# Turning the rows of a second FFN's Strassen groups back in single pieces, and reordering its last weight splits and output groups

## The chip, the cores and the metric

The kernel runs on one core of one Trainium2 chip. The metric is the device time of one execution in microseconds. The work is spread over TensorE (PE; its weight loads are shown apart as PEld), VectorE (DVE), ScalarE (ACT), GpSimd (POOL) and SyncE (SP), which issues most of the DMAs. Each engine runs its own instructions strictly in the order in which the program wrote them, and waits on semaphores for the others.

## The reference, cut to what matters

One decoder layer over 512 tokens of width 1024: a gated FFN, a mixer of attention branches, a second gated FFN, a norm. All in float32. The change is in the second FFN (`norm_ffn2`, `ffn2_gate`, `ffn2_up`, `ffn2_down`, width 2816) and the final norm.

```python
def _rmsnorm(x, g):
    xf = x.astype(jnp.float32)
    y = xf * lax.rsqrt(jnp.mean(xf * xf, axis=-1, keepdims=True) + RMS_EPS)
    return (y * g.astype(jnp.float32)).astype(x.dtype)

def _swiglu(x, w_gate, w_up, w_down):
    return (jax.nn.silu(x @ w_gate) * (x @ w_up)) @ w_down
...
        h = h + FFN_HALF * _swiglu(_rmsnorm(h, norm_ffn2[i]), ffn2_gate[i], ffn2_up[i], ffn2_down[i])
    return _rmsnorm(h, norm_final)
```

## The kernel before

**Products.** A float32 product is three matmuls on rounded (`fp32r`) halves: each operand is split into a high part, a cast on ACT, and a low part, the operand minus the high part, on DVE. The three matmuls are high x high, high x low, low x high.

**Weights.** `Weights` streams all weights in blocks of 128 x 1024. `load` (L143, SP's queue) brings a block into one of four `raw` buffers, free once the block four before it is split. `high` (L151, ACT) and `low` (L155, DVE) split it into one of four slots of `whi` and `wlo`, free once the matmuls of the block four before it are done. `next` hands out block i and, ahead of its matmuls, issues the split of block i + 2; `prep(n)` issues all splits up to block n.

**The second FFN** (L1755 on) has 22 tiles of 128 hidden columns in three parts: tiles 0 to 7, 8 to 16, 17 to 21. Most tiles compute gate and up with 24 matmuls each (`mm3`), then `gated` (Silu(gate) x up). Tiles 8 to 11, 12 to 15 and 17 to 20 are done four at a time by `four`: a Strassen scheme of seven products in the order `FOUR_ORDER` = 1, 5, 6, 3, 7, 2, 4, each of two weight blocks, 12 matmuls a block, with sums of earlier products added as each ends. After the first and second part, `down` multiplies by the down weights, again by Strassen, in 14 steps of one weight block; its left operands are seven matrices a pair of tiles, four of them sums, stored split in `G` (high) and `left` (low). The last part's down product is `finish`: four row tiles of two output groups (three for the last), each a sum of six products with the last six weight blocks, called 0 to 5 here, in the order 0, 1, 4, 5, 2, 3; then the final norm and the output.

**Turning back.** `four` leaves its result with tokens on the partitions, in tiles `s` (list `u`, first token half) and `t` (list `w`, second half); the down product needs hidden columns there. So PE transposes them into PSUM banks `tp` (`turned`) and ACT copies them out. A group hands what is left of this to the list `turns`, and `turn_back` issues one entry at chosen places in what follows. For a group whose result goes to `down`: `pair_rows(u)` is issued at the group's end, and three entries remain: `pair_rows(w)`, then `operands_of(0)` and `operands_of(1)`, each of which forms four sums in the tile `g` (L1918 to L1921) and splits them and one more matrix (L1922 to L1925). For the last group, four entries `whole(n)` each turn and split one tile. `later` holds gating operations (L1850) that are issued after the next `W.next()`.

**Three places** are named in what follows. *Seam 1*: from the end of the group of tiles 8 to 11 through the first products of the group of tiles 12 to 15. *Seam 2*: from the end of that group through tile 16 into `down`. *Tail*: the end of the group of tiles 17 to 20, tile 21, and `finish`. PSUM has two banks each of `acc`, `o`, `s` and `tp`. Blocks 0 and 1 of the last six have storage of their own (`apart`); blocks 2 to 5 take the ring's slots.

In the main loop (L2055 on), a plain tile 21 ran `next(last)` (one step of `finish`) ahead of its gate product and again after its up product:

```python
                if third == 2:
                    settle(later)
                    next(last)
                pg = acc(False)
                ...
                mm3(pu, W.next(), u_in, KD, rows if f == 0 else (lambda: back(third)) if third else None)
```

Of the kernel before, what the change touches and what calls it, by code (L numbers as in the profile page):

```python
# [195 lines left out]
def flat(t):  # L196
    return t.rearrange("p a b -> p (a b)")
# [165 lines left out]
def layer(ctx, tc, a, out):  # L363
# [335 lines left out]
    def mm3(ps, w, x, n, amid=None):  # L699
        (wh, wl), (xh, xl) = w, x  # L700
        for k in range(n):
            if amid is not None and k == n * 3 // 4:
                amid()
            mm(ps, wh[:, k], xh(k), k == 0, False)
            mm(ps, wh[:, k], xl(k), False, False)
            mm(ps, wl[:, k], xh(k), False, k == n - 1)
# [1045 lines left out]
    with pool("temp3", 2) as temp, pool("end") as end:  # L1752
# [24 lines left out]
        def gated(pg, pu, j, pairs):  # L1777
            z = temp.tile([128, S], F32, name="z")
            vector.tensor_tensor(z, pg, r_b, op=OP.mult)
            s = temp.tile([128, S], F32, name="s")  # L1780
            scalar.activation(s, z, AF.Silu)
            t = temp.tile([128, S], F32, name="t")
            vector.tensor_tensor(t, pu, r_b, op=OP.mult)
            if not pairs:
                g = temp.tile([128, 8, 256], F32, name="g", bufs=1).rearrange("p m c -> p (m c)")[:, :S]
                vector.tensor_tensor(g, s, t, op=OP.mult)
                split(*rows_of(j), g)
                return
            if j % 2 == 0:
                left["g"] = temp.tile([128, 8, 256], F32, name="g", bufs=1)  # L1790
            g, p = left["g"], j // 2
            o = g[:, 1:3] if j % 2 else g[:, 0:8:7]
            vector.tensor_tensor(o, *(x.rearrange("p (i c) -> p i c", i=2) for x in (s, t)), op=OP.mult)
            if j % 2 == 0:
                return
            if j == 7:
                W.prep(W.pos + 3)
            operands(g, p)
# [34 lines left out]
        def four(j, pairs):  # L1833
# [1 line left out]

            home = {1: "acc", 2: "acc", 5: "s", 3: "s", 6: "o", 7: "o", 4: "o"}
            slot = {5: 0, 7: 1, 6: 2, 3: 3}
            p, u, w, z = [], [], [], []
            made = {1: (p, "z"), 5: (w, "t"), 6: (u, "s"), 2: (z, "y")}
            col, minus = norm["col"], norm["minus"]  # L1840
            banks = {}
# [10 lines left out]
            for m in FOUR_ORDER:  # L1852
# [3 lines left out]
                for kk in range(2):  # L1856
                    wh, wl = (x.rearrange("p (a b) c -> p a (b c)", a=2) for x in W.next())
                    settle(later)
                    for t in range(2):
                        c, ps = slice(t * 128, t * 128 + 128), banks[home[m]][t]  # L1860
                        for k in range(2):
                            ah, al = (x[:, c] for x in operand(m, 2 * kk + k))
                            for step, (x, y) in enumerate(((ah, wh), (al, wh), (ah, wl))):
                                tensor.matmul(ps, x, y[:, k], start=new and kk == k == step == 0,  # L1864
                                              stop=kk == k == 1 and step == 2, skip_group_check=True)
                    if m == 1 and kk == 1 or m == 5:
                        turn_back()
                if m == 3:
                    next(steps, None)
                if m == 3 and not pairs:  # L1870
# [27 lines left out]
                    tensor.transpose(ps[:, i], x[:, n * 128:n * 128 + 128], ident)  # L1898
                return ps

            def pair_rows(x, first):

                banks = [turned([(x[t], 2 * q + n) for n in range(2) for t in range(2)]) for q in range(2)]
                for q, ps in enumerate(banks):
                    scalar.copy(x[q], flat(ps))
                if first:
                    for q, ps in enumerate(banks):
                        hi, lo = (y[:, j // 2 + q, 0:2] for y in (left_hi, left["lo"]))
                        scalar.copy(flat(hi), x[q])
                        vector.tensor_tensor(flat(lo), x[q], f32(flat(hi)), op=OP.subtract)  # L1910

            def operands_of(q):

                hi, lo = left_hi[:, j // 2 + q], left["lo"][:, j // 2 + q]
                a11, a12 = u[q][:, :256], u[q][:, 256:]
                a21, a22 = w[q][:, :256], w[q][:, 256:]
                g = temp.tile([128, 8, 256], F32, name="g", bufs=1)
                vector.tensor_tensor(g[:, 3], a21, a22, op=OP.subtract)  # L1918
                vector.tensor_tensor(g[:, 5], a11, a21, op=OP.subtract)
                vector.tensor_tensor(g[:, 4], g[:, 3], a11, op=OP.subtract)  # L1920
                vector.scalar_tensor_tensor(g[:, 6], a12, -1.0, g[:, 4], op0=OP.mult, op1=OP.subtract)  # L1921
                scalar.copy(hi[:, 2], a22)  # L1922
                scalar.copy(hi[:, 3:7], g[:, 3:7])
                vector.tensor_tensor(lo[:, 2], a22, f32(hi[:, 2]), op=OP.subtract)
                vector.tensor_tensor(lo[:, 3:7], g[:, 3:7], f32(hi[:, 3:7]), op=OP.subtract)  # L1925

            def whole(n):
                ps = turned([(x, n) for x in (*u, *w)])
                split(*rows_of(j + n), flat(ps))

            if pairs:
                pair_rows(u, True)
                turns.append(lambda: pair_rows(w, False))
                for q in range(2):
                    turns.append(lambda q=q: operands_of(q))
            else:
                for n in range(4):
                    turns.append(lambda n=n: whole(n))
# [45 lines left out]
        def residual(d):  # L1984
# [3 lines left out]
                tensor.transpose(ps[:, t], h[:, d, t * 128:(t + 1) * 128], ident)  # L1988
            scalar.copy(o_t[:, :, d * 128:(d + 1) * 128], ps)

        def finish():


            W.prep(base + 1)
            W.load(base + 5)
            yield
            for j in (4, 5, 2):
                W.split(base + j, 0, 8)
            yield
# [1 line left out]
            for t in range(4):  # L2001
# [3 lines left out]
                last = len(groups) - 2  # L2005
                for half, (c0, c1) in enumerate(zip(groups, groups[1:])):
                    cs = slice(c0, c1)
                    ps = acc(False)[:, :c1 - c0]
                    for n, b in enumerate(LAST_ORDER):
                        j = LAST_ROWS[b]  # L2010
                        wh, wl = (w.rearrange("p k c -> p (k c)")[:, cs] for w in W.place(base + b))
                        gh, gl = (x[:, ts] for x in rows_of(j))
                        mm(ps, gh, wh, n == 0, False)
                        mm(ps, gl, wh, False, False)
                        mm(ps, gh, wl, False, n == 5)
                    y = o_t[:, t, cs]
                    vector.scalar_tensor_tensor(y, ps, 0.5, y, op0=OP.mult, op1=OP.add)
                    sq = temp.tile([128, 512], F32, name="z")
# [41 lines left out]
        for third, (f0, f1) in enumerate(TILES):  # L2060
            if third == 2:
                make_room_again()
            for f in range(f0, f1):
                if any(x <= f < x + 4 for x in FOURS):
# [2 lines left out]
                        next(steps, None)  # L2067
                        turn[0] = 2
                    continue
                if third == 2:  # L2070
                    settle(later)
                    next(last)
                pg = acc(False)
                wp = W.next()
                settle(later)
                mm3(pg, wp, u_in, KD, col if f == 0 else None)
                back(third)
                pu = acc(False)
                mm3(pu, W.next(), u_in, KD, rows if f == 0 else (lambda: back(third)) if third else None)
                if f < 2:  # L2080
                    for d in range(4 * f, 4 * f + 4):
                        residual(d)
                if f == 1:
                    make_room()
                if third == 2:
                    next(last)
                if third < 2 and f + 1 == f1:
                    W.prep(W.pos + 2)
                if third:
# [35 lines left out]
```

## Time and profile before

| | us |
|---|---|
| median of 3 runs | 1125.27 (1123.21 to 1126.33) |
| the profiled execution's own time | 1124.9 |
| its span | 1123.2 |
| mean granted TensorE clock | 0.993 |
| chain that ended last, PE's share | 89% |

The span runs from the first to the last instruction that the profiler saw; the execution's time is 1.7 us longer. In the table of stretches the granted clock is a share of full speed. In a timeline, a matmul's length is modelled and overlaps the next one; the step from start to start (0.227 to 0.233 us for 512 columns at full clock) is its cost. A bracket `[1.90 <-ACT whi L151]` says that the engine was idle for 1.90 us before the row and that ACT's instruction of line 151 on `whi` ended it.

### The profile page before, as it was taken

The page shows a single profiled execution, that of the slowest core. Times are in us where ns is not written, and L with a number is a line of the kernel's source. Part 1 is how long each engine was busy: PE and PEld are TensorE (multiplying, and loading weights), DVE is VectorE, ACT ScalarE, POOL GpSimd, SP SyncE. Part 2 cuts the span into 40 slices and gives each one's busy share as a digit, 9 for nine tenths or more (in the row PEclk, how much of TensorE's full clock was granted, in tenths as well). Part 3 has the DMA queues.
Part 4 walks back from the last instruction along what each step waited for, and adds up shares of the span by engine and source line. Part 5 has one row for each costly group of instructions (what it writes and reads, how often), then busy time and mean ns, then how long its engine had stood idle before and what let it go on. Part 6 is the DMA issues. An engine that isn't in the chain of part 4 may idle for free.

```text
span 1123.2 us, 15782 instructions
## 1 busy us (share of the span) xinstructions
PE 1097.0 (98%) x5835; PEld 935.7 (83%) x5835; DVE 753.5 (67%) x1360; ACT 527.1 (47%) x966; POOL 213.3 (19%) x245
## 2 busy tenths in 40 slices
PE   9999999999999999999999999999999998999987
PEld 7888899988888998898888888888887786777866
DVE  5656777854656588977777466555778767587653
ACT  5433344542434457667667543434345445444432
POOL 0211110000002136645434432131100000000002
PEclk9999999999999999999999999999999999999999
DMA  7988979798656464459979756439998655445612
GB/s 213 258 207 229 237 173 267 227 315 263 210 193 188 104 188 125 139 151 242 320 164 332 173 165 207 123 97 249 266 253 259 203 172 152 148 150 190 204 38 76
DMA packets 203205, 220.90 MB, mean 197 GB/s; under 512 B 7700, under 2 KB 160088, under 8 KB 202840
## 3 DMA queue, kind: packets, MB, share of 16 engines
q1 hardware_dynamic: 177208, 156.84, 45.4%
q0 software_dynamic: 23456, 58.72, 22.7%
q10 hardware_dynamic: 2464, 4.33, 1.0%
q8 instruction: 46, 0.75, 0.3%
q14 instruction: 31, 0.25, 0.1%
HBM read 199.94 MB, written 78.64 MB: 248 GB/s over the span
## 4 chain that ended last, share of the span: by engine, by line
PE 89%; DVE 5%; ACT 3%; issue 2%; DMA 0%; POOLq 0%; DVEq 0%; ACTq 0%; SPq 0%
PE acc L387 30%; PE o L387 20%; PE s L387 20%; PE o L1864 3%; PE o L783 3%; PE s L1864 2%; PE acc L1864 2%; PE tp L1640 2%; PE s L783 2%; PE acc L783 2%; DVE wlo L155 1%; ACT whi L151 1%; PE tp L387 1%; DVE turn_a L1338 0%; DMA raw<-in_cmp_k_w_dram 0%
## 5 line engine op out<-in xcount | busy, mean ns | idle before, releaser
L155 DVE TENSOR_TENSOR wlo<-raw,whi 128x1024 fp32r<-128x1024 f32 (+2 forms) x219 | 252.0, 1173 | 61.3 <-ACT whi L151 61.0
L151 ACT CAST whi<-raw 128x1024 fp32r<-128x1024 f32 (+2 forms) x244 | 222.1, 937 | 102.2 <-PE acc L387 17.4
L387 PE MATMUL acc<-uh,whi 128*128 128x512 f32 x240 | 96.0, 400 | 0.0
L387 PE MATMUL acc<-uh,wlo 128*128 128x512 f32 x240 | 93.9, 391 | 0.0
L387 PE MATMUL acc<-ul,whi 128*128 128x512 f32 x240 | 93.7, 391 | 0.0
L387 PE MATMUL acc<-whi,uh 128*128 128x256 f32 x224 | 65.8, 294 | 1.2 <-ACT whi L151 1.2
L387 PE MATMUL acc<-wlo,uh 128*128 128x256 f32 x224 | 63.6, 284 | 0.1
L387 PE MATMUL acc<-whi,ul 128*128 128x256 f32 x224 | 63.6, 284 | 0.0
L387 PE MATMUL o<-uh,whi 128*128 128x512 f32 x144 | 57.4, 399 | 0.6 <-ACT whi L927 0.6
L1655 DVE TENSOR_TENSOR pts<-tp,pts 128x512 fp32r<-128x512 f32 (+1 forms) x62 | 41.9, 687 | 21.6 <-ACT pts L1652 21.0
L387 PE MATMUL o<-ul,whi 128*128 128x512 f32 x144 | 56.2, 390 | 0.0
L387 PE MATMUL o<-uh,wlo 128*128 128x512 f32 x144 | 56.1, 390 | 0.0
L387 PEld LDWEIGHTS acc<-uh,wlo 128*128 128x128 f32 x240 | 45.0, 188 | 10.2 <-DVE wlo L155 0.4
L2025 POOL TENSOR_TENSOR o_t<-o_t,g_b 128x512 f32<-128x512 f32 (+1 forms) x5 | 5.9, 1179 | 243.6 <-ACT z L2019 243.6
L387 PEld LDWEIGHTS acc<-ul,whi 128*128 128x128 f32 x240 | 45.2, 188 | 8.2
L387 PEld LDWEIGHTS acc<-uh,whi 128*128 128x128 f32 x240 | 45.1, 188 | 8.1
L1554 ACT ACTIVATE pbuf<-s,m 128x256 f32<-128x256 f32 (+3 forms) x96 | 47.6, 503 | 7.6 <-DVE c L1564 3.7
L387 PE MATMUL acc<-G,whi 128*128 128x512 f32 x164 | 50.5, 389 | 0.0
L387 PE MATMUL s<-uh,whi 128*128 128x512 f32 x128 | 49.9, 390 | 0.0
L387 PE MATMUL s<-ul,whi 128*128 128x512 f32 x128 | 49.8, 389 | 0.0
L387 PE MATMUL s<-uh,wlo 128*128 128x512 f32 x128 | 49.8, 389 | 0.0
L387 PE MATMUL s<-G,whi 128*128 128x512 f32 x160 | 49.4, 390 | 0.0
(468 smaller groups left out, 2936.2 us busy)
## 6 DMA issues: line engine op xcount, KB each, us to landing
raw<-in_ffn_gate_dram SPq DMA_DIRECT2D x42, 512.0 KB, 5.0
raw<-in_ffn_down_dram SPq DMA_DIRECT2D x34, 512.0 KB, 5.4
raw<-in_ffn_up_dram SPq DMA_DIRECT2D x32, 512.0 KB, 7.6
t<-in_ffn_down_dram POOLq DMA_DIRECT2D x12, 1024.0 KB, 10.0
w<-in_ffn_up_dram POOLq DMA_DIRECT2D x12, 1024.0 KB, 11.3
raw<-w SPq DMA_DIRECT2D x24, 512.0 KB, 4.0
raw<-in_w_in_dram SPq DMA_DIRECT2D x20, 512.0 KB, 5.1
raw<-s SPq DMA_DIRECT2D x16, 512.0 KB, 5.7
```

The source lines that it names most:

```text
L151: self.nc.scalar.copy(self.place(i)[0][:, k0:k1], self.raw[i][:, k0:k1])
L155: engine.tensor_tensor(lo, self.raw[i][:, k0:k1], f32(hi), op=OP.subtract)
L387: tensor.matmul(out, lhsT, rhs, start=start, stop=stop)
L783: tensor.matmul(o, a_[:, n], x(k), start=new and n == step == 0, stop=n == 7 and step == 2, skip_group_check=True)
L1554: scalar.activation(u.p[:, hd], b.view[:, j], AF.Exp, bias=u.m[:, hd:hd + 1], scale=-1.0, accum_out=u.sum[:, hd:hd + 1])
L1640: tensor.transpose(ps[:w, hd], u.p[:, hd, kb * w:kb * w + w], ident)
L1655: vector.tensor_tensor(p.lo, flat(b.ps)[:w], f32(p.hi), op=OP.subtract)
L1864: tensor.matmul(ps, x, y[:, k], start=new and kk == k == step == 0, stop=kk == k == 1 and step == 2, skip_group_check=True)
L2025: gpsimd.tensor_tensor(y, y, left["g_b"][:, cs], op=OP.mult)
```

## The change

It does seven things, all in the second FFN. (1) Nothing is turned at a group's end any more. All of a group's turning becomes six entries of `turns`: `first_rows`, `second_rows`, and for each half `sums` and `parts_of_sums`. (2) A group of `four` takes one entry after every weight block of its first three products, six in all, where it took one after product 1 and two in product 5. (3) The turned `t` goes to tiles `y` instead of over its source, and both halves' sums lie in one tile `g`. (4) Tile 16 takes entries after two and six of eight k steps of its gate product, and one and two in its up product. (5) `gated` multiplies in place in `s`. (6) Blocks 0 and 1 of the last six are split at the end of the last group's product 4, ahead of its adds and Silus; blocks 4, 5 and 2 ahead of tile 21's up product instead of after it; two `whole` entries stand in the up product apart. (7) The first row tile's two output groups run five of six products each before either runs its sixth.

```diff
@@ mm3
-            if amid is not None and k == n * 3 // 4:
+            if isinstance(amid, dict):
+                amid.get(k, int)()
+            elif amid is not None and k == n * 3 // 4:
                 amid()
@@ gated
-                g = temp.tile([128, 8, 256], F32, name="g", bufs=1).rearrange("p m c -> p (m c)")[:, :S]
-                vector.tensor_tensor(g, s, t, op=OP.mult)
-                split(*rows_of(j), g)
+                vector.tensor_tensor(s, s, t, op=OP.mult)
+                split(*rows_of(j), s)
@@ four
-                    if m == 1 and kk == 1 or m == 5:
+                    if m in FOUR_ORDER[:3]:
                         turn_back()
+                    if m == 4 and kk == 1 and not pairs:
+                        W.prep(base + 1)
...
-            def pair_rows(x, first):
+            def rows_back(x, to):
                 banks = [turned([(x[t], 2 * q + n) for n in range(2) for t in range(2)]) for q in range(2)]
                 for q, ps in enumerate(banks):
-                    scalar.copy(x[q], flat(ps))
...
+                    scalar.copy(to[q], flat(ps))
+            def operands_in(q, a, b, x):
+                hi, lo = (flat(y[:, j // 2 + q, a:b]) for y in (left_hi, left["lo"]))
+                scalar.copy(hi, x)
+                vector.tensor_tensor(lo, x, f32(hi), op=OP.subtract)
+            def first_rows():
+                rows_back(u, u)
+                for q in range(2):
+                    operands_in(q, 0, 2, u[q])
+            def second_rows():
+                back_rows.extend(temp.tile([128, S], F32, name="y") for _ in range(2))
+                rows_back(w, back_rows)
+                back_rows.append(temp.tile([128, 8, 256], F32, name="g", bufs=1))
+            def sums(q):
...
+                operands_in(q, 2, 3, a22)
+            def parts_of_sums(q):
+                operands_in(q, 3, 7, flat(back_rows[2][:, 4 * q:4 * q + 4]))
...
             if pairs:
-                pair_rows(u, True)
-                turns.append(lambda: pair_rows(w, False))
+                turns.extend((first_rows, second_rows))
                 for q in range(2):
-                    turns.append(lambda q=q: operands_of(q))
+                    turns.extend((lambda q=q: sums(q), lambda q=q: parts_of_sums(q)))
@@ finish
+        def products(ps, ts, cs, terms):
...
-            W.prep(base + 1)
             W.load(base + 5)
-            yield
             for j in (4, 5, 2):
                 W.split(base + j, 0, 8)
             yield
...
-                    ps = acc(False)[:, :c1 - c0]
...
+                    ps = groups_ps.pop(0) if groups_ps else acc(False)[:, :c1 - c0]
+                    if t == half == 0:
+                        groups_ps.append(acc(False)[:, :512])
+                        products(ps, ts, slice(0, 512), range(5))
+                        products(groups_ps[0], ts, slice(512, 1024), range(5))
+                    products(ps, ts, cs, (5,) if t == 0 else range(6))
@@ main loop
-                if third == 2:
-                    settle(later)
-                    next(last)
...
-                mm3(pg, wp, u_in, KD, col if f == 0 else None)
-                back(third)
+                mm3(pg, wp, u_in, KD, col if f == 0 else {2: turn_back, 6: turn_back} if third == 1 else None)
+                if third == 2:
+                    back(2)
+                    next(last)
                 pu = acc(False)
-                mm3(pu, W.next(), u_in, KD, rows if f == 0 else (lambda: back(third)) if third else None)
+                mm3(pu, W.next(), u_in, KD, rows if f == 0 else {2: turn_back, 6: lambda: back(3 - third)} if third else None)
...
-                if third == 2:
-                    next(last)
```

`products` holds the loop body that stood in `finish`: three matmuls for each of the terms asked for.

*Seam 1 on DVE, before*, from product 4's adds (`z<-o,z`) of the first group on; `wlo` rows are weight splits, `left` rows low parts of the down product's operands:

```order
L1891 TENSOR_TENSOR z<-o,z 128x512 x2
L1910 TENSOR_TENSOR left<-s,G 128x512 x2
L155 TENSOR_TENSOR wlo<-raw,whi 128x1024
L1850 SCALAR_TENSOR_TENSOR t<-t,minus,z 128x512 x2
L155 TENSOR_TENSOR wlo<-raw,whi 128x1024 x2
L1918 TENSOR_TENSOR g<-t 128x256
L1919 TENSOR_TENSOR g<-s,t 128x256
L1920 TENSOR_TENSOR g<-g,s 128x256
L1921 SCALAR_TENSOR_TENSOR g<-s,g 128x256
L1924 TENSOR_TENSOR left<-t,G 128x256
L1925 TENSOR_TENSOR left<-g,G 128x1024
L155 TENSOR_TENSOR wlo<-raw,whi 128x1024
```

The same place with the change:

```order
L1894 TENSOR_TENSOR z<-o,z 128x512 x2
L155 TENSOR_TENSOR wlo<-raw,whi 128x1024
L1851 SCALAR_TENSOR_TENSOR t<-t,minus,z 128x512 x2
L1913 TENSOR_TENSOR left<-s,G 128x512 x2
L155 TENSOR_TENSOR wlo<-raw,whi 128x1024 x2
L1929 TENSOR_TENSOR g<-y 128x256
L1930 TENSOR_TENSOR g<-s,y 128x256
L1931 TENSOR_TENSOR g<-g,s 128x256
L1932 SCALAR_TENSOR_TENSOR g<-s,g 128x256
L1913 TENSOR_TENSOR left<-y,G 128x256
L155 TENSOR_TENSOR wlo<-raw,whi 128x1024
L1913 TENSOR_TENSOR left<-g,G 128x1024
```

The gates of `t` moved ahead of the low parts of `s`, a weight split moved between a half's sums and their low part, and behind the last row shown now stand product 5's adds and another split before the second half's sums begin, which before followed the last row shown at once.

*Seam 2 on DVE, before*, from the first half's sums' low part to the read of tile 16's gate (`z<-acc,r_b`):

```order
L1925 TENSOR_TENSOR left<-g,G 128x1024
L155 TENSOR_TENSOR wlo<-raw,whi 128x1024
L1779 TENSOR_TENSOR z<-acc,r_b 128x512
L1783 TENSOR_TENSOR t<-o,r_b 128x512
L1786 TENSOR_TENSOR g<-s,t 128x512
L391 TENSOR_TENSOR G<-g,G 128x512
L1918 TENSOR_TENSOR g<-t 128x256
```

The same place with the change:

```order
L1913 TENSOR_TENSOR left<-g,G 128x1024
L1929 TENSOR_TENSOR g<-y 128x256
L1930 TENSOR_TENSOR g<-s,y 128x256
L1931 TENSOR_TENSOR g<-g,s 128x256
L1932 SCALAR_TENSOR_TENSOR g<-s,g 128x256
L1913 TENSOR_TENSOR left<-y,G 128x256
L155 TENSOR_TENSOR wlo<-raw,whi 128x1024
L1781 TENSOR_TENSOR z<-acc,r_b 128x512
```

The second half's sums moved from behind tile 16's gating to ahead of the read of its gate.

*The tail on ACT, before*, from the Silus of product 4 (`z<-z,rcol`) on; `G<-tp` are turned rows, `s<-z` is tile 21's Silu:

```order
L1892 ACTIVATE z<-z,rcol 128x512 x2
L151 CAST apart<-raw 128x1024 x2
L390 CAST G<-tp 128x512 x4
L151 CAST whi<-raw 128x1024 x3
L1781 ACTIVATE s<-z 128x512
L390 CAST G<-g 128x512
L151 CAST whi<-raw 128x1024
```

The same place with the change:

```order
L151 CAST apart<-raw 128x1024 x2
L1895 ACTIVATE z<-z,rcol 128x512 x2
L390 CAST G<-tp 128x512 x2
L151 CAST whi<-raw 128x1024 x3
L390 CAST G<-tp 128x512 x2
L1783 ACTIVATE s<-z 128x512
L390 CAST G<-s 128x512
L151 CAST whi<-raw 128x1024
```

The splits of blocks 0 and 1 moved ahead of the Silus, those of blocks 4, 5 and 2 ahead of half of the turned rows; block 3 stays last.

More of the change, by code (lines that the diff above doesn't have):

```diff
@@ L1837, in four @@
             slot = {5: 0, 7: 1, 6: 2, 3: 3}
-            p, u, w, z = [], [], [], []
+            p, u, w, z, back_rows = [], [], [], [], []
             made = {1: (p, "z"), 5: (w, "t"), 6: (u, "s"), 2: (z, "y")}
@@ L1899, in turned @@
                 return ps
-            def pair_rows(x, first):
+            def rows_back(x, to):
                 banks = [turned([(x[t], 2 * q + n) for n in range(2) for t in range(2)]) for q in range(2)]
                 for q, ps in enumerate(banks):
[L1905 to L1910, printed above, removed]
@@ L1912, in operands_of @@
-            def operands_of(q):
-                hi, lo = left_hi[:, j // 2 + q], left["lo"][:, j // 2 + q]
-                a11, a12 = u[q][:, :256], u[q][:, 256:]
[L1916 to L1925, printed above, removed]
+                    scalar.copy(to[q], flat(ps))
@@ new lines, in sums @@
+            def sums(q):
+                a11, a12 = u[q][:, :256], u[q][:, 256:]
+                a21, a22 = back_rows[q][:, :256], back_rows[q][:, 256:]
+                g = back_rows[2][:, 4 * q:4 * q + 4]
+                vector.tensor_tensor(g[:, 0], a21, a22, op=OP.subtract)
+                vector.tensor_tensor(g[:, 2], a11, a21, op=OP.subtract)
+                vector.tensor_tensor(g[:, 1], g[:, 0], a11, op=OP.subtract)
+                vector.scalar_tensor_tensor(g[:, 3], a12, -1.0, g[:, 1], op0=OP.mult, op1=OP.subtract)
+                operands_in(q, 2, 3, a22)
@@ L1989, in residual @@
             scalar.copy(o_t[:, :, d * 128:(d + 1) * 128], ps)
+        def products(ps, ts, cs, terms):
+            for n in terms:
+                b = LAST_ORDER[n]
+                j = LAST_ROWS[b]
+                wh, wl = (w.rearrange("p k c -> p (k c)")[:, cs] for w in W.place(base + b))
+                gh, gl = (x[:, ts] for x in rows_of(j))
+                mm(ps, gh, wh, n == 0, False)
+                mm(ps, gl, wh, False, False)
+                mm(ps, gh, wl, False, n == 5)
+        groups_ps = []
         def finish():
-            W.prep(base + 1)
             W.load(base + 5)
-            yield
             for j in (4, 5, 2):
@@ L2007, in finish @@
                     cs = slice(c0, c1)
-                    ps = acc(False)[:, :c1 - c0]
[L2009 to L2015, printed above, removed]
+                    ps = groups_ps.pop(0) if groups_ps else acc(False)[:, :c1 - c0]
[4 more added lines that the diff above has]
+                    products(ps, ts, cs, (5,) if t == 0 else range(6))
                     y = o_t[:, t, cs]
```

## The prediction, made before the changed kernel ran

> **What bounds the kernel now.** I read the page's busy times first, then a table of stretches, then the list of waits, then the timelines of the three places that these point to; a timeline row gives start, length, engine, line, operation and count, and in brackets the idle time before it and what ended that. The page and the table of stretches (columns: stretch, length, busy time and instruction count of PE, PEld, DVE, ACT, POOL, granted clock, DMA share, GB/s):
>
> ```profile
> PE 1097.0 (98%) x5835; PEld 935.7 (83%) x5835; DVE 753.5 (67%) x1360; ACT 527.1 (47%) x966; POOL 213.3 (19%) x245
> ...
> 921.40:956.20 34.80, 30.80 (x137) 23.95 (x136) 25.86 (x36) 18.85 (x25) 0.00 (x0) 1.00 0.51 155
> 967.20:990.40 23.20, 20.42 (x89) 16.18 (x88) 15.27 (x26) 11.64 (x18) 0.00 (x0) 0.93 0.31 101
> 990.40:1063.00 72.60, 72.60 (x313) 58.48 (x312) 52.83 (x60) 30.82 (x33) 0.00 (x0) 1.00 0.60 193
> 1075.70:1090.20 14.50, 10.75 (x37) 7.36 (x37) 8.48 (x11) 5.27 (x8) 1.28 (x1) 0.88 0.00 0
> ```
>
> TensorE sets the time: 98% busy, and full in long stretches. In the second FFN it loses time in three places only: **seam 1** (921.4 to 956.2), **seam 2** (967.2 to 990.4) and the **tail** (1075.7 to 1090.2). The change touches exactly these. In the list of waits PE's longest after 920 us are on ACT's and DVE's weight splits and on one DVE read (the rows at 943.78, 984.59 and 1083.33 below), none on a DMA: DVE and ACT deliver late there.
>
> **Seam 1.** The chain of waits gives the undisturbed pace of a product, 24 matmuls in 5.60; the timelines of PE, DVE and ACT give the rest:
>
> ```profile
> 893.92 5.60 PE o L1864 x24
> ...
> 921.45 1.03 PE L1898 MATMUL tp<-ident,s 128*128 128x128 f32 x8
> 922.24 0.47 PE L1864 MATMUL acc<-whi,uh 128*128 128x512 f32 x1
> 943.78 0.47 PE L1864 MATMUL s<-whi,fhi 128*128 128x512 f32 x1 [1.90 <-ACT whi L151]
> 956.25 0.39 PE L1864 MATMUL acc<-whi,uh 128*128 128x512 f32 x1
> ...
> 926.51 1.22 DVE L155 TENSOR_TENSOR wlo<-raw,whi 128x1024 fp32r<-128x1024 f32 x1 [0.18 <-ACT whi L151]
> 927.65 1.41 DVE L1850 SCALAR_TENSOR_TENSOR t<-t,minus,z 128x512 f32<-128x512 f32 x2
> 934.20 0.42 DVE L1918 TENSOR_TENSOR g<-t 128x256 f32<-128x256 f32 x1
> 935.66 0.42 DVE L1924 TENSOR_TENSOR left<-t,G 128x256 fp32r<-128x256 f32 x1
> 936.86 1.23 DVE L1925 TENSOR_TENSOR left<-g,G 128x1024 fp32r<-128x1024 f32 x1 [0.78 <-ACT G L1923]
> 942.95 1.28 DVE L1880 TENSOR_TENSOR t<-s,z 128x512 f32<-128x512 f32 x2
> ...
> 922.18 1.34 ACT L1892 ACTIVATE z<-z,rcol 128x512 f32<-128x512 f32 x2 [3.40 <-DVE z L1891]
> 930.03 1.08 ACT L1905 COPY t<-tp 128x512 f32<-128x512 f32 x2 [2.59 <-PE tp L1898]
> 930.99 1.09 ACT L1878 COPY z<-acc 128x512 f32<-128x512 f32 x2
> ```
>
> From the first transpose (921.45) to product 2 (956.25) are 34.8 us. The work is 16 transposes (2 x 0.79, from 921.45 to 922.24) and five products (5 x 5.60), 29.6. So 5.2 us are lost: the second transposes stand behind gated `t` (927.65 + 1.41), and then both halves of the sums run back to back on DVE (934 to 943), with weight splits queued behind them; the largest hole, 1.90 before 943.78, is product 3 waiting for its weights.
>
> After the change no arithmetic is removed; it is dealt out. I walk the engines in the new order. The first weight block of product 1 runs 921.45 to 924.2, transposes of `s` to 925.0, its second block to 927.7, transposes of `t`. Those need gated `t`: its Silu ends at 923.5 as now, the cast of product 5's first block follows (1.05), its low part, then the two gates, which end at 927.1: 0.6 early. ACT's copies of `t` no longer overwrite their source, so they wait for one bank only (about 928.3); then the two copies of product 1 (0.95 later, as 930.03 to 930.99), the next cast (0.95 later again, about 1.05 long), and DVE splits product 6's first block at 931.4, needed at 934.1. From here DVE has, in each product time, two splits (1.14 each, start to start), five small operations (934.20 to 936.08, 1.9), a 1024-wide low part (1.15) and two adds (1.2): 6.5 against PE's 5.60. The lead shrinks by 0.9 a product: low parts come 1.9 us ahead of the third matmul that reads them in product 6, 1.1 in product 3, 0.3 in product 7; after that only adds and splits are left (3.5 in 5.60) and it recovers. The raw loads of these blocks are issued as the slot four blocks back is split, over 5 us ahead. **Seam 1: minus 5.2**, bounds 5.2 (no hole) and 2.2 (the lead short by 1 us in each of three products).
>
> **Seam 2.** PE, ACT and DVE, and two stretches for the clock:
>
> ```profile
> 974.80 0.98 PE L1898 MATMUL tp<-ident,t 128*128 128x128 f32 x7 [0.27 <-DVE t L1850]
> 984.59 0.70 PE L387 MATMUL acc<-whi,G 128*128 128x512 f32 x1 [1.94 <-DVE z L1779]
> 990.44 0.40 PE L387 MATMUL s<-whi,G 128*128 128x512 f32 x1
> ...
> 967.88 1.34 ACT L1892 ACTIVATE z<-z,rcol 128x512 f32<-128x512 f32 x2 [3.40 <-DVE z L1891]
> 975.71 1.07 ACT L1905 COPY t<-tp 128x512 f32<-128x512 f32 x2 [3.55 <-PE tp L1898]
> 983.85 0.68 DVE L1779 TENSOR_TENSOR z<-acc,r_b 128x512 f32<-128x512 f32 x1
> ...
> 984.60:988.00 3.40, 3.40 (x8) 2.72 (x9) 2.58 (x5) 1.53 (x3) 0.00 (x0) 0.52 0.48 159
> 943.60:947.00 3.40, 2.29 (x9) 1.61 (x10) 3.40 (x5) 1.96 (x3) 0.00 (x0) 1.00 0.21 14
> ```
>
> Here the hole is a PSUM bank: the down projection's first product takes both `acc` banks, and tile 16's gate lies in one until DVE reads it at 983.85. That read stands behind the sums. Now it comes 8.14 us after the copies of `t` (975.71). In the new order the transposes of `t` stand after tile 16's sixth k step. The gates follow Silu (969.2), a cast (1.05), its low part (1.14) and themselves take 1.41, so they end near 972.8 (now 974.8), and the copies start near 973.5, 2.2 earlier. But the second half of the sums (five small operations, 1.8) now stands ahead of the read too, where now it came behind. So the read comes at 973.5 + 8.14 + 1.8 = 983.4, only 0.4 earlier. PE reaches the bank sooner, waits 2.2 instead of 1.94, and goes on 0.4 earlier. **Seam 2: minus 0.4**, bounds 0 and 2.1. The wide bound is the clock: after the hole it stood at 0.52 for 3.4 us, and 18 matmuls took 5.85 (984.59 to 990.44) instead of 4.20, 1.65 lost. After the hole of 1.90 in seam 1 it stayed at 1.00. I keep the loss, since the new hole is no shorter.
>
> The Trainium skill, page "TensorE: Matmul & The Clock Gate", section "HAM oscillation — how this bites in real kernels", asks for no idle gap above about 3.4 us if the clock is to stay up; by it the 2.2 us hole costs nothing at the clock. This trace disagrees, with 0.52 after a hole of 1.94.
>
> **Tail.** The chain of waits, then PE, ACT, DVE, one raw load's issue and the raw loads' time to landing:
>
> ```profile
> 1094.52 4.15 PE s L387 x18
> ...
> 1068.49 0.38 PE L1898 MATMUL tp<-ident,s 128*128 128x128 f32 x2
> 1075.74 1.56 PE L387 MATMUL s<-apart,G 128*128 128x512 f32 x6
> 1083.33 0.92 PE L387 MATMUL s<-whi,G 128*128 128x512 f32 x2 [3.10 <-ACT whi L151]
> 1090.21 1.56 PE L387 MATMUL o<-apart,G 128*128 128x512 f32 x6
> ...
> 1058.38 1.99 ACT L151 CAST whi<-raw 128x1024 fp32r<-128x1024 f32 x2
> 1075.08 2.96 ACT L151 CAST whi<-raw 128x1024 fp32r<-128x1024 f32 x3
> 1063.06 1.28 DVE L1891 TENSOR_TENSOR z<-o,z 128x512 f32<-128x512 f32 x2
> 1066.09 2.36 DVE L155 TENSOR_TENSOR apart<-raw,apart 128x1024 fp32r<-128x1024 f32 x2
> 1079.60 0.68 DVE L1779 TENSOR_TENSOR z<-acc,r_b 128x512 f32<-128x512 f32 x1
> ...
> 1054.20 0.34 SPq L143 DMA_DIRECT2D raw<-in_ffn_down_dram  x1
> DMA to landing us min/median/max: 3.7/4.3/5.0
> ```
>
> The first two output groups are 36 matmuls; at the pace of an undisturbed group (4.15 for 18) they need 8.3, and took 14.5 (1075.74 to 1090.21): 6.2 lost, of it 0.9 at the low clock. PE waits for blocks 4, 5, 2 (cast only after tile 21's last matmul) and then for block 3, whose cast stands behind tile 21's whole gating.
>
> New order: blocks 0 and 1 are split in ACT's gap before product 4 ends (cast from 1060.3, as the casts of 1058.38 end; the first load is issued at 1054.20 and landed by 1059.2 at the slowest). On DVE their low parts (2.36) push product 4's adds from 1063.06 to 1065.3; the gates end 2.9 after the adds begin, so at 1068.2, still ahead of the transposes at 1068.49. What queues behind is just those adds, Silus and gates; the cover is PE's gate product of tile 21, and 0.3 is left of it. The loads of blocks 4 and 5 go out 3 us sooner, as they wait for these low parts, so blocks 4, 5, 2 are cast from 1070.1, three casts in 2.96, and split by 1074.7. The turned rows follow, the last at 1075.9. Tile 21's gate is read at 1075.9 instead of 1079.60, 3.7 sooner, so block 3's halves, which PE got from 1083.33 to 1084.6, are there by 1080.8. PE now has 30 matmuls of both groups (6.9 us) from 1075.7 before it needs block 3, at 1082.6. No hole, no low clock. **Tail: minus 6.2**, bounds 6.2 and 3 (loads at 5 us plus a late chain).
>
> Using `s` in place of `g` in the gating, and four more ACT rows and two more DVE rows as pieces, cost nothing beyond what is counted above. POOL and SP keep their order.
>
> **Sum.** 5.2 + 0.4 + 6.2 = 11.8 against the profiled execution's 1124.9 (span 1123.2): 1113.1. The median of the three runs is 1125.27, 0.4 above it, so I say **1113.4**.
>
> **Rivals.**
> - *The clock stays up in seam 2.* Two holes of nearly one length (1.90, 1.94) went two ways here, so which side the new one falls on is open. Worth 1.65: 1111.7. Against it: the new hole is the longer. Chance 0.27. The rule of the Trainium skill above, taken alone, gives this case.
> - *Seam 1 is only half cured.* For it: a lead of 0.3 in product 7, and DVE over its share for two products. Worth 1 to 3: 1114.4 to 1116.4. Chance 0.16.
> - *The tail keeps part of its hole*, because loads or the gates come over the 0.3 of cover: 3 us less, 1116.4, up to the change doing nothing there, 1119.6. Chance 0.08.
> - *Slower.* Each of six pieces a group puts on DVE a wait for an ACT cast, with the next weight split behind it. Now DVE waits 2.3 (the row below, from the list of waits), 0.8 and 0.8 (936.86) a group at such places, 3.9. If six pieces wait w each, both seams cost 2 x (6w - 3.9) more, against the tail's 6.2: slower from w = 1.17; at 2.3 it is +13.6, 1138.5. Against it: ACT is busy 18.9 of 34.8 us in seam 1, and I find two waits of 0.8 and one of 1.9 there. Chance 0.03.
>
> ```profile
> DVE left L1910 <- ACT G L1909: 4.6, 2, 2.3
> ```
>
> **How the numbers follow.** Forecast as summed: 0.46; rivals 0.27, 0.16, 0.08, 0.03. The range runs over the forecast, the first two rivals and half of the third, with 1 us of scatter at the low end (the runs before span 1123.21 to 1126.33): **1110.6 to 1117.4**. A difference below 0.3% (3.4 us) can't be told from none here; all cases but the slower one and the tail doing nothing beside a seam not cured lie beyond it: faster 0.94, same 0.03, slower 0.03.
>
> **What would show it.** Right: no PE wait on `whi` or `wlo` from the first transposes of `s` to product 2, about 29.6 us; one PE wait of some 2 us on DVE's read of tile 16's gate, and the low clock after it; 8.3 us for the first 36 output matmuls, and nothing at low clock there. Wrong: a hole in product 3 or 7, a wait of transposes for gates in tile 21, blocks 4, 5, 2 waiting on DMA, or the read of tile 16's gate far from 0.4 earlier.

## The result, and the profile after

| | before | after |
|---|---|---|
| median | 1124.84 (1123.21 to 1126.33, 4 runs) | 1111.42 (1110.28 to 1112.71, 4 runs) |
| profiled execution, its span | 1124.9, 1123.2 | 1110.5, 1108.8 |
| mean granted TensorE clock | 0.993 | 0.999 |
| chain that ended last, PE's share | 89% | 93% |

Times are in us. The ratio of the two kernels' runs is 0.9881, 95% interval 0.9862 to 0.9901: 13.4 us faster; the forecast was 1113.4. The page's busy line of the changed kernel, and its whole list of PE's waits from 880 us on (total, times, longest):

```profile
PE 1091.2 (98%) x5835; PEld 933.5 (84%) x5835; DVE 753.6 (68%) x1360; ACT 526.2 (47%) x966; POOL 213.1 (19%) x245
...
PE acc L387 <- DVE z L1781: 2.0, 1, 2.0
PE tp L1901 <- DVE t L1851: 0.3, 1, 0.3
```

The shares barely move; the list of waits does. Of the waits at both seams and in the tail, two are left, both in tile 16. The table of stretches over the same places (stretch, length, busy time of PE, PEld, DVE, ACT, POOL, granted clock, DMA share, GB/s):

```profile
920.43:950.07 29.64, 29.64 (x138) 24.19 (x137) 25.42 (x36) 18.89 (x26) 0.00 (x0) 1.00 0.54 170
960.95:982.15 21.20, 18.88 (x89) 15.04 (x88) 16.07 (x27) 12.46 (x19) 0.00 (x0) 1.00 0.33 112
982.15:1054.75 72.60, 72.60 (x314) 58.48 (x312) 51.88 (x59) 31.73 (x34) 0.00 (x0) 1.00 0.59 193
1067.50:1075.79 8.29, 8.29 (x38) 6.76 (x36) 4.41 (x7) 2.20 (x3) 0.00 (x0) 1.00 0.00 0
```

PE is busy throughout seam 1 and throughout the first 36 output matmuls; the stretch between seam 2 and the tail is 72.60 as before. DVE and ACT do the same work in seam 1 (25.42 and 18.89, before 25.86 and 18.85), spread over 29.64 in place of 34.80. From the starts of PE's rows in the two timelines:

| stage | before | after | gain | forecast |
|---|---|---|---|---|
| seam 1, to product 2 | 34.80 | 29.64 | 5.16 | 5.2 |
| seam 2, to the third product of `down` | 23.29 | 21.20 | 2.09 | 0.4 |
| tail, 36 output matmuls | 14.47 | 8.29 | 6.18 | 6.2 |
| all else (span less these) | 1050.64 | 1049.67 | 0.97 | 0 |

The last row's 0.97 lies far ahead of the change: seam 1 begins at 921.45 before and at 920.43 after. Most of it is one stretch of low clock in the attention branches, of before:

```profile
472.72:476.14 3.42, 1.63 (x14) 1.34 (x11) 3.22 (x11) 2.57 (x11) 1.94 (x2) 1.00 0.00 0
476.14:479.55 3.41, 3.41 (x21) 3.14 (x20) 2.52 (x12) 2.40 (x11) 2.52 (x3) 0.50 0.00 0
```

The same code in the changed kernel's profile had no low clock there (1.00 from 471 to 478 us). One and the same matmul starts at 475.42 before and 475.71 after, ahead of that stretch; behind it another starts at 479.54 and 478.38. So the low clock cost 1.45 there, and small differences elsewhere, more than half of them in the first 7 us, give back 0.48. The change touches nothing there, so this 0.97 is no part of its gain; the experiments on the clock show why such a stretch comes and goes.

The rows that the prediction named, in the changed kernel, from the timelines of PE, DVE and ACT:

```profile
977.86 0.50 PE L387 MATMUL acc<-whi,G 128*128 128x512 f32 x1 [2.05 <-DVE z L1781]
978.20 0.39 PE L387 MATMUL acc<-whi,left 128*128 128x512 f32 x1
...
943.27 2.35 DVE L155 TENSOR_TENSOR wlo<-raw,whi 128x1024 fp32r<-128x1024 f32 x2
977.12 0.68 DVE L1781 TENSOR_TENSOR z<-acc,r_b 128x512 f32<-128x512 f32 x1
1071.25 1.22 DVE L155 TENSOR_TENSOR wlo<-raw,whi 128x1024 fp32r<-128x1024 f32 x1 [0.26 <-ACT whi L151]
...
1061.79 2.96 ACT L151 CAST whi<-raw 128x1024 fp32r<-128x1024 f32 x3
```

The hole of seam 2 is 2.05 (2.2 was forecast), but behind it the matmuls go on at full pace: from 977.86 to the third product they take 4.29, before 5.85. Block 3's low part ends at 1072.47, and PE comes to it at 1074.88.

### The profile page after: what moved, and what is told of

The parts are those of the page before. It is cut to its first block, busy times and chain, and to the rows that moved or that the text cites. A ratio compares the mean times of both kernels' runs of the same rounds, so it can differ in the third digit from the quotient of the medians.

```text
span 1108.8 us, 15781 instructions
## 1 busy us (share of the span) xinstructions
PE 1091.2 (98%) x5835; PEld 933.5 (84%) x5835; DVE 753.6 (68%) x1360; ACT 526.2 (47%) x966; POOL 213.1 (19%) x245
## 4 chain that ended last, share of the span: by engine, by line
PE 93%; DVE 4%; ACT 1%; issue 1%; DMA 1%; POOLq 0%; ACTq 0%; SPq 0%; DVEq 0%
PE acc L387 30%; PE o L387 21%; PE s L387 21%; PE o L1865 4%; PE s L1865 3%; PE acc L1865 3%; PE o L785 3%; PE tp L1642 2%; PE s L785 2%; PE acc L785 2%; DVE wlo L155 1%; PE tp L387 1%; DMA raw<-in_cmp_k_w_dram 1%; DVE turn_a L1340 0%; ACT whi L151 0%
```

## The experiments

Each was timed beside runs of the kernel before on the same chip. "Lost" is against the changed kernel's 29.64, 21.20 and 8.29 in the stages of the table above.

### The two halves of the change, and the change again

*The tail alone*: points (6) and (7) put on the kernel before.

```diff
+                    if m == 4 and kk == 1 and not pairs:
+                        W.prep(base + 1)
...
+                if third == 2:
+                    next(last)
                 pu = acc(False)
```

> The kernel before with points 6 and 7 of the change alone (splits of the last six blocks moved, first two output groups interleaved); turning of both Strassen groups as before. Theory (three places add up): seams 1 and 2 stay as before (34.8 and 23.3 us from first transposes to product 2, and from the end of group 12's product 4 to the third step of the down product), the first 36 output matmuls take 8.3 us instead of 14.5: 6.2 us faster than before, ratio 0.9945. Rival (the tail's gain depends on the seams, because loads or splits are late when the seams are): less than 4 us gained, a PE wait left between tile 21 and the second output group.

Measured 1118.59 (1117.71 to 1119.62), ratio 0.9943 (0.9927 to 0.9959). The 36 output matmuls took 8.29, and the seams kept their waits: 1.91 and 0.93 in seam 1, 1.95 in seam 2. The tail's 6.2 is its own. Seam 1 took 36.33 (919.30 to 955.63), 1.53 more than before: here its waits were followed by a stretch of low clock, from 943.69.

*The turning alone*: the changed kernel without points (6) and (7), which puts the tail's order back.

```diff
-                    if m == 4 and kk == 1 and not pairs:
-                        W.prep(base + 1)
...
+            W.prep(base + 1)
             W.load(base + 5)
+            yield
...
-                        products(ps, ts, slice(0, 512), range(5))
-                        products(groups_ps[0], ts, slice(512, 1024), range(5))
-                    products(ps, ts, cs, (5,) if t == 0 else range(6))
```

> The kernel before with points 1 to 5 alone (turning in six pieces); last splits and output groups as before. Theory: seam 1 29.6 us, no PE wait in it; seam 2 with one PE wait of 2 us, 0.4 us shorter than before if the clock drops after it and 2.1 if it does not; the tail again 14.5 us: 5.6 to 7.3 us faster, ratio 0.9935 to 0.995. Rival (the pieces pay only together with the tail): a hole in the tail longer than before, gain under 4 us.

Measured 1117.18 (1116.32 to 1118.06), ratio 0.993 (0.9914 to 0.9946). Seam 1 took 29.63, seam 2 had a hole of 2.06 without low clock behind it, and the tail its hole of 3.10 with it. The gain of 8.5 is above the 5.6 to 7.3 that were expected; its interval, 6.1 to 9.7, covers most of them. The halves add up (0.9943 x 0.993 = 0.9873) to the whole within the intervals.

*The change again*, unaltered.

> The changed kernel, unaltered, for the spread of its runs and of the granted clock. Theory (after the 2 us hole in seam 2 the clock drops in some runs and not in others): the runs fall into two groups about 1.7 us apart, near 1110.4 with a mean clock of 0.998 or more and near 1112.4 with 0.996 or less, and a profile of the slower group shows the clock near 0.5 for 3.4 us behind that hole. Rival (scatter of loads early in the program): times spread without two groups and without relation to the clock.

Measured 1112.02 (1111.67 to 1112.24), ratio 0.9884 (0.9868 to 0.99): one group within 0.6, where two were expected. The profile had a hole of 2.04 without low clock behind it, but low clock at 476 us.

### The tail, undone part by part

*Six in a row*: without point (7).

```diff
-                    if t == half == 0:
-                        groups_ps.append(acc(False)[:, :512])
-                        products(ps, ts, slice(0, 512), range(5))
-                        products(groups_ps[0], ts, slice(512, 1024), range(5))
-                    products(ps, ts, cs, (5,) if t == 0 else range(6))
+                    products(ps, ts, cs, range(6))
```

> The changed kernel without point (7): the first row tile's first output group runs its six products in a row. Block 3's low part ends at 1072.47 in the profile of the changed kernel, and would be read at 1071.42: a hole of 1.05 us there, and the time 1 us longer than the changed kernel's (in the profile; a median of these runs can hardly tell it). Rival (block 3 comes sooner, or the five products ahead are not needed): no hole. In seam 2, whose hole stays at 2.05: the clock drops after it if 1.9 us of it lie in one stretch of the 3.41 us grid that this profile's other low stretches give, else not.

*Blocks 4, 5 and 2 late*: split behind tile 21's up product.

```diff
                     back(2)
-                    next(last)
...
+                if third == 2:
+                    next(last)
                 if third < 2 and f + 1 == f1:
```

> The changed kernel with the splits of blocks 4, 5 and 2 behind tile 21's up product again, the rest kept. ScalarE's casts of them then start at 1066.9, behind the last turned rows, and their low parts end at 1071.4: holes of about 0.65 at blocks 5 and 2, and tile 21's gate is read 3.75 later, so that block 3's low part comes at 1076.2 and is waited for another 0.7. In sum 1.3 us (0.7 to 2). Rival (these splits carry the tail's gain): 3 us or more come back. In seam 2 the clock drops by the grid, as in the run without point (7).

*Blocks 0 and 1 late*: no split of them at the end of product 4.

```diff
-                    if m == 4 and kk == 1 and not pairs:
-                        W.prep(base + 1)
...
+            W.prep(base + 1)
             W.load(base + 5)
```

> The changed kernel with the splits of blocks 0 and 1 put next to those of blocks 4, 5 and 2, ahead of tile 21's up product, the rest kept. Theory: their raw buffers are those that blocks 4 and 5 are loaded into, so these loads are issued only at about 1064 and 1065 and land at 1068.3 and 1069.5; ScalarE's casts of blocks 4, 5 and 2 wait for them with the last two turned rows queued behind, and TensorE waits about 4.4 us for a turned row at 1069; after a hole of that length the clock drops, 1.7 more: 6 us lost in all, the tail's whole gain. Rival (the loads are not what counts, only the engines' queues): at most 0.3 us.

| | 36 matmuls | lost | expected | median, ratio |
|---|---|---|---|---|
| six in a row | 9.52 | 1.23 | 1.05 | 1113.69, 0.9895 (0.9871 to 0.9918) |
| 4, 5 and 2 late | 9.84 | 1.55 | 1.3 | 1113.56, 0.9902 (0.9872 to 0.9932) |
| 0 and 1 late | 12.42 | 4.13 | 6 | 1115.8, 0.9915 (0.989 to 0.9939) |

The losses are taken from start to start; a bracket counts only the idle time beyond a matmul's modelled length, so the brackets add up to less. In six in a row the matmul at 1074.59 starts 1.26 behind the pair ahead of it, in place of some 0.46, and that pair started 0.31 late. The timeline rows that carry the losses, of six in a row (PE), of 4, 5 and 2 late (PE), and of 0 and 1 late (DVE, ACT, PE), each in its own fence:

```profile
1074.59 0.50 PE L387 MATMUL s<-wlo,G 128*128 128x512 f32 x1 [0.53 <-DVE wlo L155]
```

```profile
1077.12 0.50 PE L387 MATMUL s<-wlo,G 128*128 128x512 f32 x1 [0.17 <-DVE wlo L155]
1081.98 0.50 PE L387 MATMUL s<-wlo,G 128*128 128x512 f32 x1 [0.41 <-DVE wlo L155]
```

```profile
1064.10 1.23 DVE L155 TENSOR_TENSOR apart<-raw,apart 128x1024 fp32r<-128x1024 f32 x1
...
1069.40 1.99 ACT L151 CAST whi<-raw 128x1024 fp32r<-128x1024 f32 x2 [4.39 <-DMA raw<-in_ffn_down_dram]
1071.30 1.06 ACT L390 CAST G<-tp 128x512 fp32r<-128x512 f32 x2
...
1071.93 0.50 PE L387 MATMUL s<-whi,G 128*128 128x512 f32 x1 [0.97 <-ACT G L390]
1073.50 0.50 PE L387 MATMUL s<-whi,G 128*128 128x512 f32 x1 [1.06 <-DVE G L391]
```

The last fence is the instructive one. ACT stands 4.39 us before a cast because a load has not landed: that of block 5, whose raw buffer comes free with block 1's low part, at 1065.3. What PE then waits for is not the weights but the turned rows queued behind that cast. Splitting these blocks early is therefore worth most, as an earlier issue of a load. It is the theory's mechanism at less than its size: block 0's split slipped by less than I had put (to 1059 in place of 1064), so block 4's load was in time; the holes are 2.03 in sum, and low clock follows (a fence on this kernel further down). The rival, at most 0.3, is out.

### Seam 1: the places, and the lead

*Dealt out as before*, with the new tiles.

```diff
-                    if m in FOUR_ORDER[:3]:
+                    if m == 1 and kk == 1:
+                        turn_back()
+                    if m == 5:
+                        turn_back()
                         turn_back()
...
+                if j == 0:
+                    turn_back()
```

> The changed kernel with seam 1 dealt out as before: the rows of s turned at the group's end, those of t after product 1, each half's sums and their parts together after the two weight blocks of product 5; the tiles for the turned t, the common tile for both halves' sums, and seam 2's places in tile 16 stay as changed. Theory (where the pieces are issued is what counts): seam 1 loses 3.5 to 5.2 again, with the second transposes waiting for the gates and product 3 waiting for its weights; 1115.5 to 1117. Rival (the separate tiles, with their one wait less on ScalarE's copies and on the sums' tile, carry the gain): at most 2.6 is lost, 1114.6 at most.

Measured 1118.28 (1116.48 to 1119.13, 7 runs), ratio 0.9934 (0.9914 to 0.9954). Seam 1 took 35.92, 6.28 more. PE's waits there:

```profile
928.33 0.30 PE L1904 MATMUL tp<-ident,t 128*128 128x128 f32 x1 [0.58 <-DVE t L1851]
928.90 0.98 PE L1904 MATMUL tp<-ident,t 128*128 128x128 f32 x7 [0.27 <-DVE t L1851]
943.23 0.47 PE L1865 MATMUL s<-whi,fhi 128*128 128x512 f32 x1 [1.91 <-ACT whi L151]
944.87 0.80 PE L1865 MATMUL s<-wlo,fhi 128*128 128x512 f32 x1 [0.94 <-DVE wlo L155]
```

They are the old waits (1.90 and 0.93 before) at the old places, though every tile is new: the dealing out carries the gain. Only the 0.32 for a low part in product 6 has shrunk, below what the waits list. A stretch of low clock follows here (next section), as in the tail alone, whose seam 1 took 36.33: against that the new tiles saved 0.41. The median lies above the 1115.5 to 1117 that were expected, which had no low clock in them.

*The lead of product 7*: one VectorE operation of 1.14 us more.

```diff
                 operands_in(q, 3, 7, flat(back_rows[2][:, 4 * q:4 * q + 4]))
+                if j == 0 and q == 1:
+                    hi, lo = (flat(y[:, j // 2 + q, 3:7]) for y in (left_hi, left["lo"]))
+                    vector.tensor_tensor(lo, flat(back_rows[2][:, 4 * q:4 * q + 4]), f32(hi), op=OP.subtract)
```

> The changed kernel with one more VectorE operation of 1.14 us (a low part of 128x1024 formed again, the same values) at the end of seam 1's last piece, ahead of the splits of product 7. In the changed kernel the first of these ends at 944.45 and product 7's third matmul reads it at 944.93. If that lead of 0.5 (0.3 in the prediction) is all there is, TensorE waits 0.65 there (0.85 by the prediction's figure), the only new wait. Rival (the split is early by more than a product's slack, or the added operation falls into an idle stretch of VectorE): no wait. The time goes up by 0.7, too little for the medians to tell.

```profile
946.64 0.50 PE L1865 MATMUL o<-wlo,fhi 128*128 128x512 f32 x1 [0.71 <-DVE wlo L155]
```

It is the only new wait. By the starts, the split came 1.26 later against product 7 (from 1.19 ahead of its first matmul to 0.07 behind it), and the matmul that reads it 0.88 later than its step (946.64 in place of 945.76): the lead was 0.38. Seam 1 took 30.61, 0.97 more. Measured 1113.75 (1111.38 to 1113.89), ratio 0.9903 (0.9878 to 0.9927). Seam 1 is full, but some 0.4 us of VectorE work from not being so.

### The clock behind a hole

The low stretches of before begin at 476.14, 984.72 and 1083.71, and each lasts 3.41. Their distances are 149.0 and 29.0 times 3.413: they lie on one fixed grid. In the other profiles with more than one low stretch these lie whole multiples of 3.413 apart too, the one behind the last matmul included: 12.0 in the tail alone, 38.0 in the long hole below. So I cut every profile at the lines that its own low stretches give. Of before, the stretches that hold the holes of seam 1 and seam 2, with the next stretch of seam 2:

```profile
940.35:943.76 3.41, 1.53 (x7) 0.91 (x6) 2.63 (x5) 3.04 (x4) 0.00 (x0) 1.00 0.48 150
...
981.31:984.72 3.41, 1.47 (x7) 0.88 (x6) 3.15 (x4) 1.33 (x3) 0.00 (x0) 1.00 0.14 54
984.72:988.13 3.41, 3.41 (x9) 2.64 (x10) 2.58 (x6) 1.41 (x3) 0.00 (x0) 0.50 0.48 159
```

Both holes lay inside one stretch: 1.88 idle left the clock up, 1.94 took it down for the next stretch. Of the changed kernel, whose grid is given by the low stretch behind its last matmul, from 1106.21:

```profile
973.09:976.50 3.41, 2.72 (x12) 1.88 (x10) 3.38 (x7) 1.18 (x2) 0.00 (x0) 1.00 0.08 31
976.50:979.92 3.42, 2.06 (x9) 1.71 (x10) 2.63 (x5) 1.32 (x3) 0.00 (x0) 1.00 0.36 133
979.92:983.33 3.41, 3.41 (x17) 2.73 (x16) 3.15 (x4) 3.41 (x4) 0.00 (x0) 1.00 0.08 28
...
1106.21:1108.80 2.59, 0.00 (x0) 0.00 (x0) 0.00 (x0) 0.00 (x0) 0.00 (x0) 0.50 0.11 39
```

A line of the grid at 976.50 cut the hole (975.81 to 977.86) into 0.69 and 1.36, and neither stretch was idle enough. To test that, one more kernel was run: *a long hole*.

```diff
                 operands_in(q, 2, 3, a22)
+                if j == 4 and q == 1:
+                    hi, lo = (flat(y[:, j // 2, 3:7]) for y in (left_hi, left["lo"]))
+                    for _ in range(2):
+                        vector.tensor_tensor(lo, flat(back_rows[2][:, :4]), f32(hi), op=OP.subtract)
```

> The changed kernel with two more VectorE operations of 1.14 us (a low part of 128x1024 formed again, the same values) ahead of the read of tile 16's gate. The hole of seam 2 grows from 2.05 to 4.3. Theory (the clock is decided by how much of a hole falls into one stretch of a fixed grid of 3.41 us): whatever the grid's offset, at least 1.9 us of a 4.3 us hole lie in one stretch, so the clock drops after the hole in every run, to 0.50 for 3.41 us from the next line of the grid; the time is 1114.3 plus up to 1.7, about 1115 to 1116. Rival (the new order spares the clock there, whatever the grid): no low clock after the hole, and 1114.3. A rival by length alone (some length between 1.94 and 2.05 turns it off) has no place for a drop here either.

```profile
980.70 0.79 PE L387 MATMUL acc<-whi,G 128*128 128x512 f32 x1 [4.45 <-DVE z L1781]
...
977.33:980.74 3.41, 0.04 (x1) 0.04 (x1) 3.38 (x5) 0.06 (x1) 0.00 (x0) 1.00 0.00 0
980.74:984.15 3.41, 3.41 (x8) 2.74 (x9) 2.37 (x4) 2.65 (x4) 0.00 (x0) 0.50 0.47 161
```

Measured 1115.41 (1114.72 to 1117.32), ratio 0.9914 (0.9892 to 0.9936), with the low clock from the next line, as the grid has it; the low stretch behind its last matmul, from 1110.45, gives the same lines. The kernels of the other experiments that left seam 2 as changed are further draws, since each execution falls on the grid in its own way. PE's idle time is a stretch's length less PE's busy time:

| profile | hole of seam 2 | most idle in one stretch | clock of the next |
|---|---|---|---|
| the change again | 2.04 | 1.05 | 1.00 |
| turning alone | 2.06 | 1.22 | 1.00 |
| six in a row | 2.04 | 1.32 | 1.00 |
| the change | 2.05 | 1.36 | 1.00 |
| before | 1.94 | 1.94 | 0.50 |
| tail alone | 1.95 | 1.95 | 0.50 |
| dealt as before | 2.03 | 2.03 | 0.50 |
| 4, 5 and 2 late | 2.06 | 2.05 | 0.50 |
| lead | 2.06 | 2.06 | 0.50 |
| 0 and 1 late | 2.06 | 2.06 | 0.50 |
| long hole | 4.45 | 3.37 | 0.50 |

Holes of one length (2.03 to 2.06) go both ways, four times of eight each; the idle time in one stretch sorts all eleven. It is the stretch's sum that counts, not one hole: of 0 and 1 late, whose two holes in the tail were 0.97 and 1.06, neither long by itself:

```profile
1070.69:1074.10 3.41, 1.38 (x6) 0.68 (x5) 3.41 (x5) 1.68 (x3) 0.00 (x0) 1.00 0.00 0
1074.10:1077.52 3.42, 3.42 (x10) 2.69 (x9) 2.52 (x4) 2.08 (x3) 0.00 (x0) 0.50 0.00 0
```

### Without the hole

*The gate read early*: tile 16's gate is taken out of its bank right behind its product, ahead of the weight split and the sums.

```diff
+                gate = gate_of(pg) if third == 1 else None
                 pu = acc(False)
...
-                    gated(pg, pu, f - THIRDS[2][0], False)
+                    gated(pg, pu, f - THIRDS[2][0], False, gate)
```

> The changed kernel with one edit: tile 16's gate is read out of its PSUM bank right after the gate product is issued, ahead of the sums, instead of behind them. Theory (the hole of seam 2 is the bank that waits for this read): the hole of 2.05 us goes, so does the low clock behind it, seam 2 takes about 19.2 us instead of 21.2: 2 us faster than the changed kernel in its fast group, nearly 4 in its slow group, so near 1108.5 and with one group of runs only. Rival (another wait takes its place, the second half's sums or the next weight split being late by as much): under 0.7 us gained, a PE wait on a weight split or on the read of the up product.

Measured 1109.04 (1108.43 to 1110.27), ratio 0.986 (0.9842 to 0.9877). The hole is gone, seam 2 takes 18.89 (961.74 to 980.63), and PE's only wait from 880 us on is the 0.3 of the transposes. It beats both kernels: its slowest run is faster than the fastest run of the changed kernel timed beside it (1111.67).

## Why the prediction was right, and where not

- **Seam 1, 5.2: right, and for its reasons.** No wait from the transposes of `s` to product 2. The lead of low parts was forecast as 1.9, 1.1 and 0.3 in products 6, 3 and 7; the rows give 2.04, 1.25 and 0.48 (the last from 943.27 and a split of 1.18, against the matmul at 944.93), the experiment 0.38. The rival of a half cure did not come: DVE took 6.40 a product, where 6.5 was reckoned. What the forecast left out is that the old order's 34.80 holds no low clock. In the tail alone the same waits lost it and seam 1 took 36.33, so that the change is worth 5.2 or 6.7 there, by how the execution falls on the grid.
- **Seam 2, 0.4: the mis-sized term.** The read of the gate came 16.17 after the group's end in place of 16.70, 0.53 earlier (0.4 forecast); the hole is 2.05 (2.2). The step that failed is "I keep the loss, since the new hole is no shorter". It took the length of a hole as what decides the clock. What decides is how much of it one stretch of the grid holds: the two holes of before "of nearly one length" that "went two ways" differ in this, 1.88 and 1.94. So the first rival came in, at 1.56 (5.85 less 4.29) where it was priced at 1.65, and 2.09 = 0.53 + 1.56. By the grid the 1.56 is no gain of the change: a hole of this length loses the clock about every second time, and the change left it as long.
- **Tail, 6.2: right step by step.** Set 8.24 earlier, as the first output matmul is (1075.74 to 1067.50), the forecast has the casts of blocks 4, 5 and 2 from 1061.86, the last turned row at 1067.66, tile 21's gate read then, block 3 done at 1072.56. Measured: 1061.79, 1067.6, 1067.54, 1072.47. The cover for the gates ahead of the transposes is 0.27 (0.3 forecast). Undone one at a time, the three edits cost 1.23, 1.55 and 4.13. One part was read too small: of the old tail's 6.2, 0.9 was put to the low clock, but PE was busy for 3.07 of the stretch at 0.50 from 1083.71, so about 1.5. The sum of 6.2 is taken from the starts and does not hang on it.
- **Slower**, by DVE's waits for casts at each piece: not seen. DVE has none in seam 1 at a piece, and one of 0.78 in seam 2, at the low part from 973.04.
- **The sum.** 11.8 was forecast, 14.4 is the difference of the spans: 2.6 more, of which 1.56 and most of 0.97 are stretches of low clock that fell one way in one profile and the other way in the other. Between the medians it is 13.4. The old order can lose the clock behind seam 1's waits as well: it kept it in the profile of before (1.88 idle) and lost it in those of the tail alone and of dealt as before (2.28 and 2.65 idle); in the tail alone that cost 1.53. That the medians' 1.6 above the forecast comes from there is argued from these profiles; the timed runs have no trace that would show it.

## What to carry to other kernels

When deferred work has to share two engines with a stream that the bottleneck eats, put one piece of it behind each block of the stream, and reckon the lead block by block: it shrinks by what the pieces exceed the block's time, and here a lead of 0.4 us was enough. Before taking an early split for a matter of the engines' queues, look at which loads its buffer holds back. Where a short idle time of TensorE costs clock in one profile and not in another, take neither as the price: sum the idle time that can fall into one stretch, and remove the hole.

## What the runs showed of the hardware

The granted clock was 1.00 or 0.50 for whole stretches of 3.41 us that lie on one fixed grid through an execution; how the kernel falls on it differs from run to run. In the second FFN a stretch with 1.88 us of PE idle kept the clock up for the next, one with 1.94 did not. Among the other matmuls at 473 us 1.76 to 1.79 idle took it down in five profiles (the rows of before above are one) and 1.76 left it up in dealt as before, so the limit is not one number for all work. A low stretch cost 1.4 to 1.6 us where it could be measured (1.45 at 476 us, 1.53 in seam 1, 1.56 in seam 2). A few such places could make up much of the scatter: the change's own runs lie at 1110.3, 1110.5, 1112.3 and 1112.7, with mean clocks of 0.998, 0.999, 0.996 and 0.995. That is argued, since only one of them has a trace.

The Trainium skill, page "TensorE: Matmul & The Clock Gate", section "What's actually happening", has a free-running window of 3413 ns; the low stretches here agree, 149.0 and 29.0 windows apart. Its section "HAM oscillation — how this bites in real kernels" asks for no idle gap above about 3.4 us; here 1.94 us in one stretch was enough to lose the clock, and so were two gaps of 0.97 and 1.06 in one stretch.
